# Seven plain chunks instead of six ahead of the halved products, with the making of the activation halves spread anew

## The chip, the core and the metric

The kernel runs on one core of one Trainium2 chip. The metric is the device time of one execution in microseconds (us). A core has a matrix engine (TensorE, "PE" in a profile; its weight loads are "PEld"), a vector engine (VectorE, "DVE"), a scalar engine (ScalarE, "ACT"), GpSimd ("POOL") and a queue engine (SyncE, "SP") from which this kernel issues its transfers. Each engine works through its own list of instructions in order; between engines the program waits on semaphores.

## The reference, cut to what matters

One layer with 512 tokens and a model width of 1024. Four mixers write into a merged activation, and then the part that the change touches follows, a gated feed-forward network with 2816 hidden columns:

```python
x = x + merged @ w_out[l]
hn = rmsnorm(x, ffn_norm_g[l])
gu = hn @ w_up[l]                                   # 1024 -> 2 * 2816
h = jax.nn.silu(gu[..., :FFN_HIDDEN]) * gu[..., FFN_HIDDEN:]
x = x + h @ w_down[l]
return rmsnorm(x, final_norm_g)
```

## The kernel before

Activations lie with their features on the 128 partitions and the 512 tokens along the free axis. To keep single precision at the matmul's faster rate, every operand is split into a high part (a rounding copy on ScalarE, `A.copy`) and a low part (the difference, a subtraction on VectorE), and each product is three matmuls: high times high, high times low, low times high. Weights arrive in chunks of up to 128 x 2048 floats through two buffers named `raw`; while TensorE works on one chunk, ScalarE and VectorE split the next (`hi` and `lo`, or `ahi` and `alo`).

The up projection takes 22 chunks, one for each block of 128 hidden columns, in two parts of eleven (`for part in range(2)`); after each part the matching rows of `w_down` are multiplied in.

The first `N_PLAIN` chunks, six of them, are plain: `mm3` makes the gate product `psg` (tile `m_fg`) and then the up product `psu` (`m_fu`), each with 24 matmuls of 128x512. `glu_up` then scales both (`tg`, `tu`), takes the silu of `tg` on ScalarE, multiplies, and splits the result into `hh` (ScalarE) and `hl` (VectorE), which only the `w_down` products read.

All later chunks are halved: `up_halved` makes the same two products with a Strassen-like scheme from seven products of half the size, each with 12 matmuls of 128x256 (`prod`, names B11, B21, T2, T1, T3, B22 and T4, in this order). They read sums and differences of weight quarters, made by the step `sum` and its fellows in `split_steps`, and sums and differences of activation halves. B11, T2, T3 and T4 all add up in one half `ac` of a PSUM bank (tile `s_fa`); between them ScalarE copies the running sum out (`A.copy(mu[:, h0], ac)` after B11, and again after T2), so T2 may not write before the first copy is done. That copy stands on ScalarE behind the first high part of the next chunk (`emit(st, "ha")`).

The activation halves are made once, by `halves_gen`, during the plain chunks. It has twelve steps, three for each of four values of k. Step A scales two blocks of x2 (`xsa`, `xsb`; VectorE) and copies (`xsp`) and rounds (`xsh`) on ScalarE. Step B makes the differences (two `xst`, two `xsu`) and one low part (`xsl`) on VectorE, and rounds two tiles on ScalarE. Step C makes the other low parts, two for even k and three for odd k. Where the steps stand is set by hand: each plain chunk from the third on takes one (`next(prep)`) between its two products, and then `PREP[j]` more behind its `glu_up`. B11, the first half-size product, reads the last low part of the last step C.

There is no scheduler: the engines' order is the order of the Python code (`tc.manual_schedule()`), and helper calls all carry line 81, so the rows below are told apart by their tiles. The prediction names chunks by j, from 0: the last plain chunk is 5 before.

Of the kernel before, what the change touches and what calls it, by code (L numbers as in the profile page):

```python
# [14 lines left out]
ALU = mybir.AluOpType  # L15
# [41 lines left out]
N_WARM = 8  # L57
N_HALVED = 2
BC_AT = 7
PREP = (0, 1, 2, 1, 2, 2)  # L60
N_PLAIN = 6
W0_PIECES = {0: 1, 1: 3, 4: 2, 6: 2}
S5_PAR = 48
S5_W = S5_PAR + 4 * 256
# [21 lines left out]
def _advance(clock, key, cost):  # L86
    clock[key] = cost + (clock[key] if key == "pe" else max(clock[key], clock["pe"]))
# [3 lines left out]
def hybrid_trunk(ctx: ExitStack, tc: tile.TileContext, a: dict, out: bass.AP):  # L91
# [3 lines left out]
    V = _Paced(nc.vector, lambda n: _advance(clock, "v", 0.09 + 1.04e-3 * n))  # L95
    A = _Paced(nc.scalar, lambda n: _advance(clock, "a", 0.20 + 0.83e-3 * n))
# [16 lines left out]
    def nm_(nm):  # L113
        uid[0] += 1
        return f"{nm}_{uid[0]}"

    def slot(nm):
        return sp.tile([P, T], F32, tag="s", name=nm_(nm))
# [5 lines left out]
    def main_ps(nm):  # L124
        return pm.tile([P, T], F32, tag="mm", name=nm_("m_" + nm))

    def side_ps(nm):
        return pa.tile([P, T], F32, tag="at", name=nm_("s_" + nm))

    def r_(t):  # L130
        return t.bitcast(F32R)

    def split(src, nm, mk=None):
        mk = mk or slot
        hi = mk(nm + "h")
        lo = mk(nm + "l")
        A.copy(r_(hi), src)
        V.tensor_tensor(r_(lo), src, hi, ALU.subtract)
        return r_(hi), r_(lo)
# [13 lines left out]
    for part in range(2):  # L153
        specs += [
            ("w_up", j, 2048) if j < N_PLAIN else ("w_ups", j - N_PLAIN, 2048)
            for j in range(NH // 2 * part, NH // 2 * (part + 1))
# [77 lines left out]
    def emit(steps, *names):  # L234
        for n in names:
            for f in steps.pop(n, ()):
                f()

    def flush(steps):
        for n in ("ha", "la", "sum", "ha2", "la2", "sum4", "hb", "lb", "hc", "lc", "ld"):  # L240
            emit(steps, n)

    def open_chunk():
        c = used[0]
        used[0] += 1
        while len(loaded) < min(len(ready) + N_RAW, len(specs)):
            load_next()
        steps = {}
        if len(ready) < min(c + 2, len(specs)):
            steps = split_steps()  # L250
        return ready[c], steps
# [24 lines left out]
    def mm3(ps, ch, c, nw, acts, k0=0):  # L276
        n = len(acts)
        for k, (ah, al) in enumerate(acts):
            wh, wl = ch.h(k0 + k, c, P, nw), ch.l(k0 + k, c, P, nw)
            PE.matmul(ps, wh, ah, start=k == 0, stop=False)  # L280
            PE.matmul(ps, wh, al, start=False, stop=False)
            PE.matmul(ps, wl, ah, start=False, stop=k == n - 1)
# [90 lines left out]
    def inv_rms(ps, n):  # L373
        def s_(nm):
            return gp.tile([P, n], F32, name=nm_(nm))

        ms = s_("ms")
        V.tensor_scalar(ms, ps, 1.0 / D, EPS, ALU.mult, ALU.add)
        rt = s_("rt")
        A.activation(rt, ps, AF.Sqrt, scale=1.0 / D, bias=epsc)  # L380
        r0 = s_("r0")
        V.reciprocal(r0, rt)
        t = s_("nt")
        V.tensor_tensor(t, r0, r0, ALU.mult)
        V.scalar_tensor_tensor(t, t, -0.5, ms, ALU.mult, ALU.mult)
        r = s_("rr")
        V.scalar_tensor_tensor(r, t, 1.5, r0, ALU.add, ALU.mult)
        return r

    def diags(r, nm):  # L390
        o = []
        for b in range(4):
            dg = sm.tile([P, P], F32, tag="dg", name=nm_("dg"), bufs=4)
            V.tensor_scalar(dg, ident, r[:, b : b + 1], None, ALU.mult)
            o.append(dg)
        return o

    def bcast_rows(dgs, rb):
        ps = side_ps("bc")
        for b in range(4):  # L400
            PE.matmul(ps[:, b * P : (b + 1) * P], ones, dgs[b], start=True, stop=True)
        A.copy(rb, ps)

    def ssq_mm(acc):
        ps = side_ps("ssq")
        for b in range(4):
            PE.matmul(ps[:, b : b + 1], acc[:, b * P : (b + 1) * P], ones[:, 0:1], start=True, stop=True)
        return ps
# [7 lines left out]
    for kt in range(KT):  # L416
        hi, lo = slot("xh"), slot("xl")
# [796 lines left out]
    for c in range(4):  # L1214
        ch = next_chunk()
        for n in range(2):
# [6 lines left out]
            hi, lo = slot("x2h"), slot("x2l")  # L1223
# [7 lines left out]
    def glu_up(psg, psu):  # L1231
        tg, tu = slot("tg"), slot("tu")
        V.tensor_tensor(tg, psg, rb2, ALU.mult)
        A.activation(tg, tg, AF.Silu)
        V.tensor_tensor(tu, psu, rb2, ALU.mult)
        V.tensor_tensor(tu, tu, tg, ALU.mult)
        return split(tu, "h")

# [57 lines left out]
    def up_halved(late):  # L1298
        ch, st = open_chunk()
        pa_, pb_ = side_ps("fa"), main_ps("fb")  # L1300
        ac, b1, b2 = pa_[:, h0], pb_[:, h0], pb_[:, h1]
        mu, cn = slot("mu"), slot("cn")
        prod(ac, ch.ahi, ch.alo, 0, "B11", first=True)
        emit(st, "ha")
        late[0]()
        emit(st, "la")
        A.copy(mu[:, h0], ac)
        prod(b1, ch.ahi, ch.alo, 2, "B21", first=True)
        emit(st, "sum")
        late[1]()  # L1310
        emit(st, "ha2", "la2", "sum4")
        prod(ac, ch.hi, ch.lo, 0, "T2")
        A.copy(mu[:, h1], ac)
        prod(b2, ch.hi, ch.lo, 1, "T1", first=True)
        emit(st, "hb")
        A.copy(cn[:, h0], b2)
        emit(st, "lb")
        prod(ac, ch.hi, ch.lo, 3, "T3")
        V.tensor_tensor(cn[:, h1], ac, cn[:, h0], ALU.add)
        emit(st, "hc", "lc")  # L1320
        prod(b2, ch.hi, ch.lo, 2, "B22")
        V.tensor_tensor(mu, mu, pb_, ALU.add)
        A.activation(mu, mu, AF.Silu)
        flush(st)
        prod(ac, ch.ahi, ch.alo, 1, "T4")
        tu, hi, lo = slot("tu"), slot("hh"), slot("hl")
        hid.append((r_(hi), r_(lo)))

        def high():
            V.scalar_tensor_tensor(tu[:, h0], ac, -1.0, mu[:, h0], ALU.mult, ALU.mult)  # L1330
            V.scalar_tensor_tensor(tu[:, h1], cn[:, h1], -1.0, mu[:, h1], ALU.mult, ALU.mult)
            A.copy(r_(hi), tu)

        def low():
            V.tensor_tensor(r_(lo), tu, hi, ALU.subtract)

        return high, low

    hk = NH // 2
    for part in range(2):  # L1340
        hid = []
        late = (lambda: None,) * 2
        for j in range(hk * part, hk * (part + 1)):
            if j >= N_PLAIN:
                late = up_halved(late)
                continue
            ch, st = open_chunk()
            emit(st, "ha", "la")
            if "sum" not in st:
                flush(st)  # L1350
            psg = main_ps("fg")
            mm3(psg, ch, 0, 256, x2g)
            if j == 1:
                bcast_rows(dgs, rb2)
                hid.append(glu_up(*first))
                prep = halves_gen()
            if j > 1:
                next(prep)
            emit(st, "sum", "ha2", "la2", "sum4", "hb", "lb")
            psu = side_ps("fu") if j < 2 else main_ps("fu")  # L1360
            mm3(psu, ch, P, 256, x2g)
            if j == 0:
                dgs = diags(inv_rms(ssq_mm(acc)[:, 0:4], 4), "r2")
                acc = None
                first = psg, psu
                continue
            hid.append(glu_up(psg, psu))
            for _ in range(PREP[j]):
                next(prep)
            flush(st)  # L1370
        for nt in range(8 - N_HALVED * part):
            if nt == 0:
                ch, st = open_chunk()
                emit(st, "ha")
                late[0]()
                late[1]()
                flush(st)
            else:
                ch = next_chunk()
            ps = main_ps("d")  # L1380
            mm3(ps, ch, 0, P, hid)
            V.tensor_tensor(x2[nt], ps, x2[nt], ALU.add)
            if part:
                acc = sumsq_add(acc, x2[nt])
# [125 lines left out]
def _layout(inp):  # L1510
# [47 lines left out]
    for b, kts in enumerate((4, 2, 4, 4)):  # L1558
# [8 lines left out]
    up = _chunks(wu, 256)  # L1567
    o["w_up"] = up[:N_PLAIN]
    hv = up[N_PLAIN:].reshape(NH - N_PLAIN, P, 2, 4, 2, P).transpose(0, 1, 4, 2, 3, 5)
    o["w_ups"] = np.ascontiguousarray(  # L1570
        np.stack([hv[:, :, 0, 0], hv[:, :, 1, 1], hv[:, :, 0, 1], hv[:, :, 1, 0]], axis=2)
    ).reshape(NH - N_PLAIN, P, 2048)
    wd = f["w_down"][0]
# [21 lines left out]
```

## Time and profile before

| what | value |
|---|---|
| median of three runs | 986.85 us (986.72 to 987.58) |
| the profiled execution, whole | 987.47 us |
| its span, first to last instruction | 985.4 us |
| TensorE busy | 965.4 us, 98% of the span |
| VectorE busy | 661.7 us, 67% |
| ScalarE busy | 411.9 us, 42% |
| mean granted TensorE clock | 0.992 of full |

Busy shares are means over stages that differ. The time at the end is set where the engine that is nearly always busy stands still, so the list of what TensorE waited for is read first, and then the lists of instructions in order of time around that wait. In such a list each row has the start, the duration, the engine, the operation and its tiles as out<-in; what stands in brackets is idle time of that engine just ahead of the row, with the instruction that ended it. Instructions of one engine overlap a little, so that the step from one start to the next is somewhat shorter than a duration.

### The profile page before, as it was taken

The page shows a single profiled execution, that of the slowest core. Times are in us where ns is not written, and L with a number is a line of the kernel's source. Part 1 is how long each engine was busy: PE and PEld are TensorE (multiplying, and loading weights), DVE is VectorE, ACT ScalarE, POOL GpSimd, SP SyncE. Part 2 cuts the span into 40 slices and gives each one's busy share as a digit, 9 for nine tenths or more (in the row PEclk, how much of TensorE's full clock was granted, in tenths as well). Part 3 has the DMA queues.
Part 4 walks back from the last instruction along what each step waited for, and adds up shares of the span by engine and source line. Part 5 has one row for each costly group of instructions (what it writes and reads, how often), then busy time and mean ns, then how long its engine had stood idle before and what let it go on. Part 6 is the DMA issues. An engine that isn't in the chain of part 4 may idle for free.

```text
span 985.4 us, 13841 instructions
## 1 busy us (share of the span) xinstructions
PE 965.4 (98%) x5462; PEld 834.9 (85%) x5462; DVE 661.7 (67%) x1260; ACT 411.9 (42%) x718; POOL 4.3 (0%) x20
## 2 busy tenths in 40 slices
PE   8999999999999999999999999996999999999996
PEld 7887888888888888887888888885998899999886
DVE  6676676688777877945545555579883379997344
ACT  7443533343545344227333334354552235554231
POOL 1000000000000000000000000000000000000000
PEclk9999999999999999999999999999899999999998
DMA  8532222231222213251532332221223223232312
GB/s 274 182 111 97 88 89 88 68 121 37 68 77 72 69 58 111 100 192 65 182 117 96 118 128 85 86 86 44 94 94 118 102 86 129 86 123 74 110 59 86
DMA packets 38696, 100.26 MB, mean 102 GB/s; under 512 B 14222, under 2 KB 22075, under 8 KB 32872
## 3 DMA queue, kind: packets, MB, share of 16 engines
q1 hardware_dynamic: 38632, 99.38, 29.9%
q8 instruction: 43, 0.70, 0.3%
q14 instruction: 21, 0.17, 0.1%
HBM read 94.94 MB, written 4.42 MB: 101 GB/s over the span
## 4 chain that ended last, share of the span: by engine, by line
PE 94%; DVE 3%; ACT 1%; DMA 0%; issue 0%; SPq 0%; DVEq 0%
PE m_g L81 17%; PE m_d L81 12%; PE s_fa L81 9%; PE m_b L81 7%; PE m_fb L81 7%; PE m_qk L81 7%; PE m_sqk L81 4%; PE m_o L81 4%; PE m_v L81 3%; PE m_u L81 3%; PE m_fg L81 3%; PE m_sv L81 2%; PE m_fu L81 2%; PE s_u L81 1%; PE s_fu L81 1%; PE m_gb L81 1%
## 5 line engine op out<-in xcount | busy, mean ns | idle before, releaser
L81 DVE TENSOR_TENSOR lo<-raw,hi 128x1024 fp32r<-128x1024 f32 (+5 forms) x208 | 198.1, 984 | 54.8 <-ACT hi L81 53.9
L81 ACT CAST hi<-raw 128x1024 fp32r<-128x1024 f32 (+5 forms) x208 | 169.4, 858 | 64.3 <-PE m_d L81 30.0
L81 PE MATMUL m_g<-xh,hi 128*128 128x512 f32 x256 | 102.6, 401 | 0.0
L81 PE MATMUL m_g<-xh,lo 128*128 128x512 f32 x256 | 100.0, 391 | 0.3 <-DVE lo L81 0.3
L81 PE MATMUL m_g<-xl,hi 128*128 128x512 f32 x256 | 99.6, 389 | 0.0
L81 PE MATMUL m_d<-hh,hi 128*128 128x512 f32 (+1 forms) x198 | 72.5, 366 | 0.0
L81 PE MATMUL m_d<-hl,hi 128*128 128x512 f32 (+1 forms) x198 | 72.4, 366 | 0.0
L81 PE MATMUL m_d<-hh,lo 128*128 128x512 f32 (+1 forms) x198 | 72.3, 365 | 0.0
L81 ACT ACTIVATE gt<-gt 128x512 f32<-128x512 f32 x32 | 20.2, 631 | 109.7 <-DVE gt L81 109.7
L81 PEld LDWEIGHTS m_g<-xh,lo 128*128 128x128 f32 x256 | 48.0, 188 | 11.3 <-DVE lo L81 1.0
L81 PEld LDWEIGHTS m_g<-xh,hi 128*128 128x128 f32 x256 | 48.1, 188 | 10.9 <-issue 1.0
L81 PEld LDWEIGHTS m_g<-xl,hi 128*128 128x128 f32 x256 | 48.1, 188 | 10.7 <-issue 1.0
L81 DVE TENSOR_TENSOR x<-m_d,x 128x512 f32<-128x512 f32 (+1 forms) x18 | 11.4, 633 | 62.5 <-PE m_d L81 62.5
L81 PE MATMUL s_fa<-xsl,ahi 128*128 128x256 f32 x128 | 36.7, 286 | 8.6 <-DVE xsl L81 8.6
L81 DVE TENSOR_TENSOR raw<-raw 128x512 f32<-128x512 f32 (+1 forms) x48 | 41.8, 870 | 1.6
L81 PEld LDWEIGHTS m_d<-hh,lo 128*128 128x128 f32 x198 | 37.3, 189 | 6.1
L81 PEld LDWEIGHTS m_d<-hh,hi 128*128 128x128 f32 x198 | 37.3, 189 | 6.0
L81 PEld LDWEIGHTS m_d<-hl,hi 128*128 128x128 f32 x198 | 37.4, 189 | 5.9
L81 DVE TENSOR_TENSOR gt<-m_b,gt 128x512 f32<-128x512 f32 x24 | 16.5, 689 | 37.9 <-PE m_b L81 32.8
L81 ACT ACTIVATE prob<-prob,nmx 128x128 f32<-128x128 f32 (+1 forms) x48 | 20.1, 419 | 49.3 <-DVE nmx L81 49.2
L81 PE MATMUL m_qk<-xh,hi 128*128 128x512 f32 x96 | 38.2, 397 | 0.0
L81 PE MATMUL m_qk<-xl,hi 128*128 128x512 f32 x96 | 37.4, 390 | 0.0
(400 smaller groups left out, 2523.7 us busy)
## 6 DMA issues: line engine op xcount, KB each, us to landing
raw<-in_w_g SPq DMA_DIRECT2D x24, 768.0 KB, 4.3
raw<-in_w_in SPq DMA_DIRECT2D x17, 1024.0 KB, 6.8
raw<-in_w_ups SPq DMA_DIRECT2D x16, 1024.0 KB, 4.8
raw<-in_w_down SPq DMA_DIRECT2D x16, 704.0 KB, 4.0
raw<-in_w_up SPq DMA_DIRECT2D x6, 1024.0 KB, 4.8
raw<-in_w_g SPq DMA_DIRECT2D x8, 640.0 KB, 3.9
raw<-in_w_out SPq DMA_DIRECT2D x4, 1024.0 KB, 4.8
x<-in_x SPq DMA_DIRECT2D x8, 256.0 KB, 5.5
```

The costliest lines, as they stand in the source:

```text
L81: return f(out, *args, **kw)
```

## The change

Seven plain chunks stand ahead of the halved ones in place of six, so there are fifteen halved chunks, not sixteen. `PREP` is another table, the steps of `halves_gen` begin in chunk 1 and end in chunk 5, and the low part of h (`hl`) is no longer issued by `glu_up` itself: `glu_up` returns it, and it is issued behind the steps that follow.

```diff
-PREP = (0, 1, 2, 1, 2, 2)
-N_PLAIN = 6
+PREP = (0, 1, 2, 2, 1, 1)
+N_PLAIN = 7
...
         V.tensor_tensor(tu, tu, tg, ALU.mult)
-        return split(tu, "h")
+        hi, lo = slot("hh"), slot("hl")
+        A.copy(r_(hi), tu)
+        hid.append((r_(hi), r_(lo)))
+        return lambda: V.tensor_tensor(r_(lo), tu, hi, ALU.subtract)
...
             if j == 1:
                 bcast_rows(dgs, rb2)
-                hid.append(glu_up(*first))
+                low = glu_up(*first)
                 prep = halves_gen()
-            if j > 1:
+                next(prep)
+                low()
+            elif 1 < j < 6:
                 next(prep)
...
-            hid.append(glu_up(psg, psu))
-            for _ in range(PREP[j]):
+            low = glu_up(psg, psu)
+            for _ in range(PREP[j] if j < 6 else 0):
                 next(prep)
+            low()
             flush(st)
```

So the steps stand as follows (Ak, Bk, Ck for each k; what is in brackets stands between the two products of a chunk, the rest behind its `glu_up`):

| chunk j | before | after |
|---|---|---|
| 1 | A0 | A0 (ahead of the `hl` of chunk 0), B0 |
| 2 | (B0) C0 A1 | (C0) A1 B1 |
| 3 | (B1) C1 | (C1) A2 B2 |
| 4 | (A2) B2 C2 | (C2) A3 |
| 5 | (A3) B3 C3, then the first halved chunk | (B3) C3 |
| 6 | | no step, then the first halved chunk |

VectorE at the last steps, before. It begins with the product of the last plain chunk (5): `tu` and `hl` belong to `glu_up`, the nine rows from `xst` to `xsl` are B3 and C3 less their parts on ScalarE, and `lo_5891` finishes the weights of the first halved chunk:

```order
L81 TENSOR_TENSOR tu_5963<-m_fu_5937,rb_879_5442 128x512
L81 TENSOR_TENSOR tu_5963<-tu_5963,tg_5962 128x512
L81 TENSOR_TENSOR hl_5969<-tu_5963,hh_5968 128x512
L81 TENSOR_TENSOR xst_5972<-xsa_5921 128x256
L81 TENSOR_TENSOR xst_5972<-xsb_5922,xsa_5921 128x256
L81 SCALAR_TENSOR_TENSOR xsu_5973<-xst_5972,xsb_5922 128x256
L81 SCALAR_TENSOR_TENSOR xsu_5973<-xsu_5973,xsb_5922 128x256
L81 TENSOR_TENSOR xsl_5978<-xsb_5922,xsh_5926 128x512
L81 TENSOR_TENSOR xsl_5984<-xst_5972,xsh_5980 128x512
L81 TENSOR_TENSOR xsl_5986<-xsu_5973,xsh_5982 128x512
L81 TENSOR_TENSOR xsl_5988<-xsp_5833,xsh_5928 128x512
L81 TENSOR_TENSOR lo_5891<-raw_5796,hi_5890 128x512 x2
```

The same engine after, from the product of chunk 5, which is no longer the last plain one:

```order
L81 TENSOR_TENSOR tu_5968<-m_fu_5942,rb_879_5442 128x512
L81 TENSOR_TENSOR tu_5968<-tu_5968,tg_5967 128x512
L81 TENSOR_TENSOR xsl_5976<-xst_5930,xsh_5938 128x512
L81 TENSOR_TENSOR xsl_5978<-xsu_5931,xsh_5940 128x512
L81 TENSOR_TENSOR xsl_5980<-xsp_5799,xsh_5894 128x512
L81 TENSOR_TENSOR hl_5974<-tu_5968,hh_5973 128x512
L81 TENSOR_TENSOR alo_5988<-raw_5897,ahi_5987 128x1024
L81 TENSOR_TENSOR raw_5897<-raw_5897 128x2x512
L81 TENSOR_TENSOR raw_5897<-raw_5897 128x512
L81 TENSOR_TENSOR alo_5988<-raw_5897,ahi_5987 128x512
L81 TENSOR_TENSOR raw_5897<-raw_5897 128x512
L81 TENSOR_TENSOR lo_5986<-raw_5897,hi_5985 128x1024
```

The last `xsl` of C3 stands behind the product of chunk 5 in both, but chunk 5 was followed by the first halved chunk and is now followed by chunk 6; the weights of the first halved chunk (`alo`, `raw`, `lo`) now come behind all steps, and `hl` behind the low parts.

ScalarE around the end of the last plain chunk, before (`tg` is its silu, `hh` the high part of its h, `hi_5890` the last weights of the first halved chunk, `ahi_5998` the first of the second, and `mu` the copy that T2 waits for):

```order
L81 ACTIVATE tg_5962<-tg_5962 128x512
L81 CAST hh_5968<-tu_5963 128x512
L81 CAST xsh_5980<-xst_5972 128x512
L81 CAST xsh_5982<-xsu_5973 128x512
L81 CAST hi_5890<-raw_5796 128x512 x2
L81 CAST ahi_5998<-raw_5888 128x1024
L81 COPY mu_6002<-s_fa_6000 128x256
```

And after:

```order
L81 ACTIVATE tg_6048<-tg_6048 128x512
L81 CAST hh_6054<-tu_6049 128x512
L81 CAST hi_5985<-raw_5897 128x512 x2
L81 CAST ahi_6066<-raw_5983 128x1024
L81 COPY mu_6070<-s_fa_6068 128x256
```

The two roundings of step B are gone from this place; the rest stands as it stood, with `mu` behind `hh`, `hi` and `ahi`.

## Rows read from the trace of the kernel before

**Rows 1.** From the page: the span, and its instructions.
```profile
span 985.4 us, 13841 instructions
```
**Rows 2.** What TensorE waited for, whole run: us in total, times, longest us.
```profile
PE s_fa L81 <- DVE xsl L81: 8.6, 1, 8.6
```
**Rows 3.** TensorE in order of time: chunk starts, the gap, a chunk's last matmul.
```profile
669.63 0.39 PE L81 MATMUL m_fu<-x2h,lo 128*128 128x512 f32 x1
669.85 0.39 PE L81 MATMUL m_fg<-x2h,hi 128*128 128x512 f32 x1
...
680.73 0.28 PE L81 MATMUL s_fa<-xsh,ahi 128*128 128x256 f32 x1
...
681.45 0.28 PE L81 MATMUL s_fa<-xsh,ahi 128*128 128x256 f32 x1
690.30 0.58 PE L81 MATMUL s_fa<-xsl,ahi 128*128 128x256 f32 x1 [8.57 <-DVE xsl L81]
...
702.17 0.28 PE L81 MATMUL s_fa<-xsh,ahi 128*128 128x256 f32 x1
...
712.25 0.28 PE L81 MATMUL s_fa<-xsh,ahi 128*128 128x256 f32 x1
```
**Rows 4.** Stretches: length, busy us (count) of PE, PEld, DVE, ACT, POOL; PEclk, DMA, GB/s.
```profile
669.85:680.73 10.88, 10.88 (x49) 9.01 (x48) 9.81 (x16) 5.49 (x10) 0.00 (x0) 1.00 0.18 77
685.00:687.00 2.00, 0.00 (x0) 0.00 (x0) 1.33 (x4) 0.62 (x1) 0.00 (x0) 0.72 0.00 0
693.00:695.00 2.00, 2.00 (x12) 2.00 (x11) 1.97 (x3) 0.00 (x0) 0.00 (x0) 0.50 0.89 360
702.17:712.25 10.08, 10.08 (x86) 10.08 (x85) 9.24 (x14) 5.72 (x11) 0.00 (x0) 1.00 0.28 106
```
**Rows 5.** VectorE in order of time, from chunk 5 to the last step.
```profile
665.38 2.35 DVE L81 TENSOR_TENSOR lo<-raw,hi 128x1024 fp32r<-128x1024 f32 x2
...
670.05 0.69 DVE L81 TENSOR_TENSOR tu<-m_fu,rb 128x512 f32<-128x512 f32 x1 [0.39 <-PE m_fu L81]
670.85 0.69 DVE L81 TENSOR_TENSOR tu<-tu,tg 128x512 f32<-128x512 f32 x1
...
672.84 0.42 DVE L81 TENSOR_TENSOR xst<-xsa 128x256 f32<-128x256 f32 x1
...
675.51 0.68 DVE L81 TENSOR_TENSOR xsl<-xsu,xsh 128x512 fp32r<-128x512 f32 x1
676.12 1.22 DVE L81 TENSOR_TENSOR alo<-raw,ahi 128x1024 fp32r<-128x1024 f32 x1
677.25 0.74 DVE L81 SCALAR_TENSOR_TENSOR xsa<-x,cols,rb 128x512 f32<-128x512 f32 x1
...
678.57 1.95 DVE L81 TENSOR_TENSOR raw<-raw 128x1024 f32<-128x1024 f32 x2
680.44 0.69 DVE L81 TENSOR_TENSOR alo<-raw,ahi 128x512 fp32r<-128x512 f32 x1
...
682.91 0.68 DVE L81 TENSOR_TENSOR tg<-m_fg,rb 128x512 f32<-128x512 f32 x1
...
689.55 0.69 DVE L81 TENSOR_TENSOR xsl<-xsp,xsh 128x512 fp32r<-128x512 f32 x1
```
**Rows 6.** What VectorE waited for from 630 to 702 us: total, times, longest us.
```profile
DVE lo L81 <- ACT hi L81: 5.9, 3, 2.2
DVE hl L81 <- ACT hh L81: 4.1, 6, 0.7
```
**Rows 7.** ScalarE in order of time: the instructions that stand ahead of `mu`.
```profile
671.58 0.62 ACT L81 CAST hh<-tu 128x512 fp32r<-128x512 f32 x1 [1.25 <-DVE tu L81]
...
688.39 1.13 ACT L81 CAST hi<-raw 128x512 fp32r<-128x512 f32 x2
689.43 1.04 ACT L81 CAST ahi<-raw 128x1024 fp32r<-128x1024 f32 x1
691.77 0.37 ACT L81 COPY mu<-s_fa 128x256 f32<-128x256 f32 x1 [1.30 <-PE s_fa L81]
```

## The prediction

> **What bounds the kernel now.** The list of TensorE's waits comes first: the engine is busy nearly all the time, and its one long wait, 8.6 us, is that of `s_fa`, the first halved product, for a low activation half, `xsl` [rows 2]. The list of TensorE in order of time gives the place. Chunk 5 starts at 669.85 and the first halved chunk at 680.73, so a plain chunk takes 10.88 us. Seven matmuls later, at 681.45, TensorE stands still until 690.30; the next two halved chunks start at 702.17 and 712.25 [rows 3]. An undisturbed halved chunk thus takes 10.08 us and the first took 21.44: an excess of **11.36 us**. Of it 690.30 - 681.45 - 0.12 = 8.73 is the gap (0.12 is the step of these matmuls: 10.08 / 84). The other 2.63 comes after the gap: the granted clock was 1.00 in chunk 5, fell during the gap (0.72 in the mean of 685 to 687), was 0.50 at 693 to 695 while TensorE worked without a pause, and 1.00 again from 702.17 on [rows 4]. Half speed is 1.2 of 2.4 GHz.
>
> The Trainium skill, "TensorE: Matmul & The Clock Gate", section "Part 1: The HAM clock gate", says that idleness throttles TensorE to half and that activity releases it; these rows agree.
>
> The list of VectorE tells why the half is late. At 689.55 it does the last `xsl` of C3, and the matmul starts 0.06 us after that ends [rows 5]. VectorE had simply not got through its list: it was busy 9.81 of 10.88 us in chunk 5 [rows 4], and it stood idle for 4.1 us in six waits for `hh` just ahead of `hl` [rows 6].
>
> **The change, part by part.** Times are counted on the trace of before, whose order is the same up to the product of chunk 0.
>
> *The gap and its clock go, if the halves are ready.* Chunk 6 is now plain and runs from 680.73 to 691.61. The product of chunk 5 can start when its last matmul is done. In chunk 4 `tu` started 0.42 us after the last `m_fu` started (669.63 to 670.05), and the second `tu` 0.80 later [rows 3, 5]. So for chunk 5: last matmul 680.51, `tu` 680.93, second `tu` 681.73, then the three `xsl` of C3 at 0.61 each (675.51 to 676.12): done by 684.2, where the first halved product now wants them at 691.6. That is 7.4 us to spare where 8.7 were missing. Is VectorE on time at 680.93? From the `tu` of chunk 4 at 670.05: 0.80, then 0.60, then A3 at 1.32 (677.25 to 678.57) [rows 5], `hl` 0.61, and then it needs ScalarE's `hi`, which stands behind `hh` (671.58 [rows 7]) and three small copies, so that it can begin the two `lo` near 675.0; 2.35 for these, 2.07 for B3 (672.84 to 676.12 is 3.28 for B and two `xsl`, less 1.21), 0.60 for `tg`: 680.0. About 0.9 us to spare, so yes. Both halves of the excess go: **-11.36**.
>
> *A halved chunk becomes a plain one*: 10.88 - 10.08 = **+0.80**. The bytes loaded are the same; VectorE and ScalarE have less to do for it.
>
> The Trainium skill, "Perfetto Trace Analysis", section "Matmuls", holds that larger matmuls are more efficient than smaller ones. Taken alone, that would price this swap at nothing or a gain, and the sum would be 0.80 lower. The rows agree per column (48 x 512 in 10.88 us against 84 x 256 in 10.08) but the halved chunk has an eighth fewer columns, and so the measured 0.80 decides.
>
> *A new wait.* T2 may not write before `mu` has been copied, and on ScalarE `mu` stands behind `hh` of the last plain chunk, two `hi` and one `ahi`. Before, that chain was through long before TensorE woke: `mu` itself waited 1.30 us for TensorE [rows 7]. Now it starts from the end of chunk 6: last `m_fu` at 691.39, `tu` at 691.81, `hh` 1.53 us after that (670.05 to 671.58 [rows 5, 7]) at 693.34; then `hh` 0.62, two `hi` 1.04 (688.39 to 689.43), `ahi` 1.04 and `mu` 0.37 [rows 7]: `mu` is done at 696.4. TensorE has only B11 and B21 to do meanwhile, 24 matmuls at 0.12: T2 could begin at 691.61 + 2.88 = 694.5. So it waits **+1.9**. VectorE must not be late for this `tu`: after C3 (684.2) it has `hl` 0.61, `alo` 1.13 (676.12 to 677.25), the sums 1.87 (678.57 to 680.44), three more rows 2.47 (680.44 to 682.91) and `tg` 0.60 [rows 5]: 690.9, some 0.9 us early. The bounds of this wait: 1.5, if each of the four copies overlaps the next by 0.1, as the two `hi` do with `ahi` (1.13 long, 1.04 apart); 2.8, if VectorE is 0.9 late after all, its reserve lost twice over.
>
> *Behind it* VectorE begins the next `alo` at about 696.0, and T4 waits for its `cn`. An undisturbed halved chunk holds 9.24 us of VectorE work in 10.08 [rows 4]; of the 0.84 to spare a lag of this size uses up nearly all. I take **+0.1**, bounds 0 and 0.8.
>
> *Edits at nothing.* `hl` behind the steps: its readers are the `w_down` products, four halved chunks later, and steps now fill most of the 4.1 us of waiting [rows 6]; without that cover nothing changes for TensorE, which does not read it. A0 in chunk 1: VectorE has slack there. The transfers: the program issues the same loads in the same order, each when the low parts of its buffer's last chunk are done, and TensorE waits for none of them before [rows 2]; the load of the third halved chunk starts when the last `lo` of the first one is done, about when `mu` is (696), and is wanted near 704.
>
> **Sum**: -11.36 + 0.80 + 1.9 + 0.1 = -8.56. The profiled execution took 987.47 us, 2.07 more than its span [rows 1], and 0.62 more than the median of 986.85; the saving lies inside the span, so it is taken off the median: 986.85 - 8.56 = **978.3 us**. With the bounds of the two waits (1.5 + 0 to 2.8 + 0.8) the forecast's own range is 977.8 to 979.9.
>
> **The rivals.**
>
> *No new wait.* If T2 did not have to wait, because `mu` gets through earlier than this chain has it, TensorE would run on: 986.85 - 10.56 = 976.3. For it: before, nothing of the kind is among TensorE's waits [rows 2]. Against it: before, the gap hid this chain, and every row of it has a duration.
>
> *The clock falls again.* The new wait of 1.9 us could do what that of 8.73 did. Its price would be up to the 2.63 paid before: 978.3 + 2.6 = 980.9. Against it: in the one long gap the clock was still high for 4.3 us (a mean of 0.72 between 1.00 and 0.50 puts the fall near 685.9, the last matmul near 681.6) [rows 3, 4], more than twice the new wait.
>
> The page named above would make a gap that is long enough throttle the engine; whether this one is, no row here shows.
>
> *VectorE late at every plain chunk: slower than before.* The steps stand closer now. The fullest list is that from the `tu` of chunk 2 to that of chunk 3: 0.80 + 0.60, A1 1.32, B1 2.07, `hl` 0.61, `lo` 2.35, C1 1.83, `tg` 0.60 [rows 5], together 10.18, and some 0.5 of waiting for `hi`: 10.7 of the 10.88 that TensorE takes. If that waiting were the 2.2 us that it was at its longest before [rows 6], and the list 0.6 longer than its rows, VectorE would fall 2.1 us behind at each of the five boundaries from chunk 2 to 7, and the matmuls that read `lo` would wait there: 978.3 + 5 x 2.1 = 988.8. It decides from 1.7 us at each boundary (8.56 / 5), a list of 12.6 us. Against it: all of these rows have been seen at their lengths, chunks 4 and 5 have shorter lists and give back what chunk 3 loses, and the first 2 us are forgiven: `lo` was done at 667.7 for a chunk that began at 669.85 [rows 3, 5].
>
> *The change doesn't cure the wait* (the first halved chunk waits for something else that I overlook, such as its weights, for as long as before): about 986 to 987.6, no change.
>
> **How the numbers follow.** Forecast 0.77; no new wait 0.07; the clock 0.10; VectorE late 0.03; not cured 0.03. A difference of 0.2% (2.0 us) is about what a measurement of this kernel can tell from none. The first three cases, 0.94, are faster by more than that; the fourth is slower. Of the last, 0.02 falls within 0.2% and 0.01 on a small gain: faster 0.95, same 0.02, slower 0.03. The range takes in the forecast's bounds, the case without a wait and that of the clock: 976.1 to 981.0. Outside lie the last two cases, 0.06, and some tails.
>
> **What would show it.** In the profile after, `s_fa <- xsl` is gone from TensorE's waits; in its place stands one wait of about 1.9 us of `s_fa` for ScalarE's `mu`, near 694.5, and perhaps one below 0.5 us for `cn`. The seventh plain chunk runs from about 680.7 to 691.6, the granted clock stays at 1.00 through both, the second halved chunk starts near 703.6 and the third 10.08 later. A TensorE wait for `lo` or `tu` at the start of chunks 3 to 6 would show the slower rival, a clock of 0.50 behind the new wait the second, and no TensorE wait at all the first. The prediction is wrong if the first halved chunk still waits longer than 4 us for anything.

## The result, and the profile after

The kernel after took **979.50 us** in the median of four runs (978.61 to 980.17), the kernel before 986.99 us in the median of four on the same chip. The ratio is 0.9921, with a 95% interval of 0.9908 to 0.9933: 7.5 us faster by the medians, where 8.56 were forecast, and the whole interval lies below 1. The profiled execution took 980.17 us with a span of 978.4 us.

The first view is the list of what TensorE waited for in the kernel after (total us, times, longest us):

```profile
PE s_u L81 <- ACT hi L81: 2.9, 2, 1.5
PE s_fa L81 <- ACT mu L81: 1.6, 1, 1.6
```

The wait of 8.6 us for `xsl` [rows 2] is gone. In its place stands one of 1.6 us for `mu`. The other row, two waits of `s_u` (the first product of the kernel), lies in the first ten microseconds and comes up again below.

TensorE of the kernel after in order of time (start, duration, operation, idle time ahead of it and what ended that). The rows answer to [rows 3]: start of chunk 6, start of the first halved chunk, last matmul of B21, first of T2, last matmul ahead of T4, T4, and the second halved chunk.

```profile
682.34 0.39 PE L81 MATMUL m_fg<-x2h,hi 128*128 128x512 f32 x1
...
693.22 0.28 PE L81 MATMUL s_fa<-xsh,ahi 128*128 128x256 f32 x1
...
695.97 0.28 PE L81 MATMUL m_fb<-xsh,alo 128*128 128x256 f32 x1
697.87 0.39 PE L81 MATMUL s_fa<-xsh,hi 128*128 128x256 f32 x1 [1.62 <-ACT mu L81]
...
703.61 0.28 PE L81 MATMUL m_fb<-xsh,lo 128*128 128x256 f32 x1
703.74 0.29 PE L81 MATMUL s_fa<-xsh,ahi 128*128 128x256 f32 x1
...
705.17 0.28 PE L81 MATMUL s_fa<-xsh,ahi 128*128 128x256 f32 x1
```

Chunk 6 takes 693.22 - 682.34 = 10.88 us as a plain chunk. The first halved chunk runs through to B21 without a pause, then stands still ahead of T2. Chunks 6 and 7 together took 712.25 - 680.73 = 31.52 us before, both halved [rows 3]; after, one plain and one halved, they take 705.17 - 682.34 = 22.83. That is 8.69 us less.

The stretches of the kernel after (length; busy us and count of PE, PEld, DVE, ACT, POOL; granted clock; share and GB/s of the transfers), as in [rows 4]: chunk 6, the wait, the time behind it, and the second halved chunk.

```profile
682.34:693.22 10.88, 10.88 (x49) 9.01 (x48) 9.88 (x13) 4.04 (x6) 0.00 (x0) 1.00 0.12 47
...
696.00:698.00 2.00, 0.38 (x4) 0.18 (x3) 1.91 (x4) 2.00 (x5) 0.00 (x0) 1.00 0.00 0
698.00:700.00 2.00, 2.00 (x17) 2.00 (x18) 1.97 (x2) 0.71 (x2) 0.00 (x0) 1.00 0.71 213
705.17:715.25 10.08, 10.08 (x86) 10.08 (x85) 9.31 (x14) 5.77 (x11) 0.00 (x0) 1.00 0.30 104
```

The granted clock stays at 1.00, that is 2.4 GHz, through the wait and behind it. Before, it fell to 0.50 [rows 4].

VectorE of the kernel after, at the products of chunk 5 and chunk 6, and at the last `xsl` of C3:

```profile
682.54 0.69 DVE L81 TENSOR_TENSOR tu<-m_fu,rb 128x512 f32<-128x512 f32 x1 [0.47 <-PE m_fu L81]
...
685.15 0.69 DVE L81 TENSOR_TENSOR xsl<-xsp,xsh 128x512 fp32r<-128x512 f32 x1
...
693.42 0.69 DVE L81 TENSOR_TENSOR tu<-m_fu,rb 128x512 f32<-128x512 f32 x1 [0.80 <-PE m_fu L81]
```

VectorE now waits for TensorE at both products; it is on time with 0.47 and 0.80 us to spare. The last `xsl` is done at 685.84, 7.4 us ahead of the chunk that wants it.

ScalarE of the kernel after, from the last `hh` of a plain chunk to `mu`, the rows that answer to [rows 7]:

```profile
694.94 0.62 ACT L81 CAST hh<-tu 128x512 fp32r<-128x512 f32 x1 [1.59 <-DVE tu L81]
695.47 1.14 ACT L81 CAST hi<-raw 128x512 fp32r<-128x512 f32 x2
696.51 1.04 ACT L81 CAST ahi<-raw 128x1024 fp32r<-128x1024 f32 x1
697.46 0.36 ACT L81 COPY mu<-s_fa 128x256 f32<-128x256 f32 x1
```

B11 is finished at 694.8, so `mu` could have been copied then. It stands behind `hh`, two `hi` and `ahi`, which have no pause between them, and T2 follows 0.05 us after it ends.

### Where the missing microsecond is

The up projection begins with the first `m_fg`, at 613.58 in the trace of before and 615.18 in that of after. From there to the end of the span it is 371.8 us before and 363.2 after: 8.6 less, the forecast. What the profiled run lost again, 1.6 us, it lost ahead of the up projection, where the change alters nothing. TensorE at the start of the kernel after:

```profile
7.16 0.40 PE L81 MATMUL s_u<-xh,lo 128*128 128x512 f32 x1
8.95 0.50 PE L81 MATMUL s_u<-xh,hi 128*128 128x512 f32 x1 [1.40 <-ACT hi L81]
...
12.00 0.63 PE L81 MATMUL s_u<-xh,lo 128*128 128x512 f32 x1
...
20.75 0.39 PE L81 MATMUL m_u<-xh,hi 128*128 128x512 f32 x1
```

and its stretches there (columns as above):

```profile
10.00:12.00 2.00, 2.00 (x7) 1.58 (x7) 2.00 (x4) 1.94 (x4) 0.00 (x0) 0.69 1.07 411
12.00:14.00 2.00, 2.00 (x6) 1.62 (x5) 2.00 (x4) 1.94 (x4) 0.00 (x0) 0.50 1.02 405
```

TensorE begins at full pace, runs out of weights after six matmuls, stands still for 1.40 us, and soon after that works at half the clock for some 3 us. The pause alone is not what costs the time, as the last section shows. The same place in the trace of before:

```profile
6.35 0.80 PE L81 MATMUL s_u<-xh,hi 128*128 128x512 f32 x1 [1.58 <-ACT hi L81]
...
19.23 0.39 PE L81 MATMUL m_u<-xh,hi 128*128 128x512 f32 x1
```

Here the first matmuls go at half pace (the next starts 0.59 us later, those behind it 0.43 us apart), the weights are there when they are wanted, nothing runs dry, and the second chunk of weights is reached at 19.23, not 20.75.

### The profile page after: what moved, and what is told of

Read it like the earlier page. It is cut to its first block, busy times and chain, and to the rows that moved or that the text cites. A ratio compares the mean times of both kernels' runs of the same rounds, so it can differ in the third digit from the quotient of the medians.

```text
span 978.4 us, 13757 instructions
## 1 busy us (share of the span) xinstructions
PE 963.7 (99%) x5426; PEld 831.3 (85%) x5426; DVE 656.8 (67%) x1253; ACT 409.1 (42%) x712; POOL 4.3 (0%) x20
## 4 chain that ended last, share of the span: by engine, by line
PE 96%; DVE 2%; ACT 1%; DMA 1%; issue 0%; SPq 0%; DVEq 0%
PE m_g L81 17%; PE m_d L81 12%; PE s_fa L81 9%; PE m_b L81 7%; PE m_qk L81 7%; PE m_fb L81 6%; PE m_sqk L81 4%; PE m_o L81 4%; PE m_fg L81 4%; PE m_v L81 3%; PE m_u L81 3%; PE m_fu L81 3%; PE m_sv L81 2%; PE s_u L81 1%; PE s_fu L81 1%; PE m_gb L81 1%
## 5 line engine op out<-in xcount | busy, mean ns | idle before, releaser
L81 DVE TENSOR_TENSOR raw<-raw 128x512 f32<-128x512 f32 (+1 forms) x45 | 39.1, 870 | 1.6
L81 PE MATMUL m_qk<-xh,lo 128*128 128x512 f32 x96 | 37.4, 390 | 0.0
```

What stands on the lines that cost most here:

```text
L81: return f(out, *args, **kw)
```

## The experiments

The second column is the median of each run, and its ratio is to the kernel before timed beside it on the same chip. The runs stood on three chips, on which the kernel before took 987.15, 988.16 and 987.61 us in the median, so that kernels are better compared by their ratios than by their medians. "Stretch" is the time from the first `m_fg` to the end of the span in the profiled run, which leaves the start out. The kernel after in its own trace: wait for `mu` 1.62 us, stretch 363.2 us; the kernel before: 371.8 us.

| run | median us | ratio to before, 95% interval | span us | first m_fg | stretch us |
|---|---|---|---|---|---|
| again | 979.49 | 0.9918 (0.9905 to 0.9932) | 978.4 | 615.21 | 363.2 |
| e1_seven_alone | 982.54 | 0.9947 (0.9934 to 0.9960) | 978.4 | 613.29 | 365.1 |
| e2_spread_alone | 983.69 | 0.9968 (0.9956 to 0.9979) | 981.7 | 613.38 | 368.3 |
| e3_low_in_place | 983.26 | 0.9959 (0.9945 to 0.9974) | 984.1 | 615.34 | 368.8 |
| e4_mu_first | 978.45 | 0.9910 (0.9897 to 0.9924) | 977.7 | 615.26 | 362.4 |
| e5_wait_plus4 | 983.71 | 0.9960 (0.9945 to 0.9975) | 981.5 | 613.27 | 368.2 |
| e6_wait_plus8 | 985.45 | 0.9979 (0.9970 to 0.9988) | 983.0 | 612.90 | 370.1 |
| e7_longer_warm | 977.89 | 0.9901 (0.9888 to 0.9913) | 976.3 | 613.81 | 362.5 |
| e8_low_alone | 982.20 | 0.9942 (0.9926 to 0.9958) | 979.1 | 613.22 | 365.9 |
| e9_after_warm | 979.12 | 0.9910 (0.9894 to 0.9927) | 977.4 | 614.18 | 363.2 |

### The kernel after once more

> The changed kernel as it is, timed once more beside the kernel before. Theory: everything the change does lies between chunk 6 and chunk 8 of the up projection, where the two traces differ by 8.7 us; the further 1.6 us by which the profiled run of after lags lies in its first 20 us, in a part that the change does not touch, and is chance. Then the median is 978 to 979, the saving 8 to 8.8 us, and in this trace the first plain chunk starts earlier than in the first trace of after, or the same late start is seen in a run of before. Rival: the late start belongs to the changed program; then the median is near 980 and this trace again shows about 1.6 us more of TensorE waits in the first 20 us than any trace of before.

Nothing is edited. The time, the wait for `mu` (1.6 us) and the stretch repeat. The median of 979.49 lies above the 978 to 979 of the theory. The late start came again: a pause of 1.37 us at 9.00, a clock of 0.60 from 10 to 12 us, and `m_u` at 20.78. So this run does not exclude the rival that the late start belongs to the changed program. Against it stand other runs below: ahead of the up projection `e1_seven_alone`, `e5_wait_plus4`, `e6_wait_plus8` and `e8_low_alone` have the same instructions as the kernel after, and they reach `m_u` at 18.50 to 18.92.

### Seven plain chunks alone

The kernel before with two numbers and a condition changed; steps and low parts stand as before.

```diff
-PREP = (0, 1, 2, 1, 2, 2)
-N_PLAIN = 6
+PREP = (0, 1, 2, 1, 2, 2, 0)
+N_PLAIN = 7
...
-            if j > 1:
+            if 1 < j < 6:
                 next(prep)
```

> Seven plain chunks alone: the old table of steps (none in chunk 6) and the low part of h at its old place. Theory: the wait for xsl goes, since chunk 6 gives it 10.9 us, but VectorE gets to the product of chunk 6 about 2.0 us late (six waits of 0.69 for hh come back, and the weights of the first halved chunk stand behind B3 and C3), and the copy mu with it: the wait of T2 is 3.9 us instead of 1.6, and the time 2.0 to 2.5 above the changed kernel, about 981, if the clock holds. Rival (the extra chunk is all that counts): within 0.5 us of the changed kernel.

TensorE ahead of T2, in this kernel's trace:

```profile
697.94 0.39 PE L81 MATMUL s_fa<-xsh,hi 128*128 128x256 f32 x1 [3.57 <-ACT mu L81]
```

and the stretches of and behind that wait:

```profile
696.00:698.00 2.00, 0.06 (x1) 0.07 (x1) 1.91 (x4) 2.00 (x5) 0.00 (x0) 1.00 0.00 0
698.00:700.00 2.00, 2.00 (x17) 2.00 (x18) 1.97 (x2) 0.74 (x2) 0.00 (x0) 1.00 0.66 168
```

In this trace the seventh chunk alone brings 6.7 of the 8.6 us (371.8 - 365.1), close to what the theory had; the wait is a little shorter than its 3.9. Without the other edits VectorE was on time for the product of chunk 5 (it waited 0.54 us for TensorE) and did that of chunk 6 at 693.50, 1.97 us later than the kernel after does, counted from the first `m_fg`. All of that lateness goes into the wait for `mu`: 3.57 - 1.62 = 1.95, and 365.1 - 363.2 = 1.9. The clock held at 1.00 through this wait. In the other four runs the time is 1.2 to 3.3 us longer, with a mean clock of 0.994 to 0.996 in place of 0.997; they have no trace, so whether the clock fell behind this wait or in the start isn't shown. The traced run is the fastest of the five: by the medians, beside the same runs of the kernel before, the seventh chunk alone brings 4.6 us (987.15 - 982.54) where the kernel after brings 7.7 (987.15 - 979.49).

### The steps and the low parts alone

The kernel after with six plain chunks.

```diff
-N_PLAIN = 7
+N_PLAIN = 6
```

> The new table and the late low part of h alone, with six plain chunks: steps begin in chunk 1, C3 still stands behind the product of chunk 5, and the first halved chunk follows. Theory: VectorE has the last xsl at 686.3 on the clock of the trace before (tu of chunk 5 at 683.9, three xsl), so the gap at the first halved product is 4.8 us, not 8.7; nothing is paid for a plain chunk; the clock may fall just before the end of the gap. The time is 4 us below before without a fall of the clock missed in full (983), up to 6.6 below (980.3) if the clock holds. Rival (spreading does nothing without the chunk): within 0.5 us of before.

TensorE in the first halved chunk:

```profile
686.72 0.58 PE L81 MATMUL s_fa<-xsl,ahi 128*128 128x256 f32 x1 [5.20 <-DVE xsl L81]
```

and the stretches of this wait and behind it:

```profile
684.00:686.00 2.00, 0.00 (x0) 0.00 (x0) 1.90 (x5) 1.24 (x4) 0.00 (x0) 0.82 0.00 0
...
690.00:692.00 2.00, 2.00 (x11) 2.00 (x10) 1.97 (x3) 0.00 (x0) 0.00 (x0) 0.50 0.84 344
```

The wait shrinks from 8.57 to 5.20 us, 3.37 less, and the stretch by 3.5: the clock falls as before and is paid for in full. With six chunks neither of the two orders tried removes the wait. The two halves add up to 6.7 + 3.5 = 10.2, and together they bring 8.6: with the seventh chunk there is no wait for `xsl` left that the new order could shorten. In the traces it is then worth the 1.9 us of the wait for `mu` alone; by the medians it is 3.1 (7.7 - 4.6).

### The low part of h back in its place

The kernel after; the end of `glu_up` is as it was.

```diff
-        return lambda: V.tensor_tensor(r_(lo), tu, hi, ALU.subtract)
+        V.tensor_tensor(r_(lo), tu, hi, ALU.subtract)
+        return lambda: None
```

> The changed kernel with one part undone: hl stands again right behind hh, so that VectorE waits 0.69 us for it in each chunk; seven plain chunks and the new table stay. The prediction costs this edit at nothing. Theory A (VectorE's slack takes most of it): in the trace of after, VectorE had 0.79, 0.47 and 0.80 us of idle time ahead of the products of chunks 4, 5 and 6 and none ahead of that of chunk 3; 0.69 more in each list leaves it some 0.5 us late at chunk 6, the wait of T2 is 2.1 us, the time 0.5 us above the changed kernel. Rival B (what the prediction says, nothing): wait 1.6, same time. Rival C (it is this edit that keeps VectorE on time): the lateness adds up over five chunks to 2 us or more, the wait of T2 is over 3.5 us, the time 2 us or more above the changed kernel.

What VectorE waited for from 618 to 699 us in this kernel:

```profile
DVE lo L81 <- ACT hi L81: 5.4, 4, 2.2
DVE hl L81 <- ACT hh L81: 4.9, 7, 0.7
```

and in the kernel after, in the same stretch:

```profile
DVE tu L81 <- PE m_fu L81: 4.0, 4, 1.9
DVE lo L81 <- ACT hi L81: 3.0, 4, 1.6
DVE hl L81 <- ACT hh L81: 0.7, 1, 0.7
```

In place, each `hl` stands right behind the `hh` that it subtracts, and VectorE waits 0.69 us for it, seven times. Moved, it waits once. That alone is 4.2 us. Together with longer waits for `hi` (2.4) it is more than the 4.0 us that VectorE had in hand ahead of its products, and VectorE comes to the product of chunk 6 2.5 us late (696.13; the last `m_fu` starts at 693.16). So T2:

```profile
700.68 0.58 PE L81 MATMUL s_fa<-xsh,hi 128*128 128x256 f32 x1 [4.27 <-ACT mu L81]
```

and the clock:

```profile
698.00:700.00 2.00, 0.00 (x0) 0.00 (x0) 1.59 (x3) 2.00 (x4) 0.00 (x0) 0.88 0.00 0
700.00:702.00 2.00, 1.32 (x6) 1.32 (x7) 1.88 (x3) 1.15 (x3) 0.00 (x0) 0.50 0.43 53
```

So `hl` in its old place costs TensorE a good deal, as rival C had it. The stretch is 5.5 us longer than after (984.1 - 615.34 against 978.4 - 615.18): 2.65 of wait, and 2.9 lost by work at half the clock. Three of the six runs were long (984.07 to 986.12, mean clock 0.991 to 0.992), three were shorter (982.15 to 982.45, 0.995 to 0.996): the wait is there each time by its order, the fall of the clock probably not, but only the profiled run has a trace.

### The low part alone, with the old table

The kernel after, with seven plain chunks and the old table of steps.

```diff
-PREP = (0, 1, 2, 2, 1, 1)
+PREP = (0, 1, 2, 1, 2, 2, 0)
...
                 low = glu_up(*first)
                 prep = halves_gen()
-                next(prep)
                 low()
...
-            for _ in range(PREP[j] if j < 6 else 0):
+            for _ in range(PREP[j]):
```

> Seven plain chunks, the old table of steps, but hl behind the steps that follow (so the kernel after without the new table). Theory (both edits are needed): with the old table and hl in place VectorE was on time for the product of chunk 5 (it waited 0.54 us there) and 1.97 us late for that of chunk 6, since chunk 5 alone holds B3 and C3; hl behind them saves only the 0.69 us wait of that chunk, so it is still about 1.3 late, T2 waits 1.62 + 1.3 = 2.9 us for mu, and the stretch from the first row of the up projection to the end is about 363.2 + 1.3 = 364.5 us. Rival (the low part is the whole of it, the table does nothing): T2 waits 1.6 us and the stretch is 363.2. Other rival (the low part does nothing here): 3.6 and 365.1, as with seven chunks alone.

T2 in this kernel, and the stretches from its wait on:

```profile
697.13 0.39 PE L81 MATMUL s_fa<-xsh,hi 128*128 128x256 f32 x1 [2.84 <-ACT mu L81]
```

```profile
696.00:698.00 2.00, 0.87 (x5) 0.87 (x6) 1.91 (x3) 1.60 (x3) 0.00 (x0) 0.89 0.16 25
698.00:700.00 2.00, 2.00 (x12) 2.00 (x11) 1.93 (x4) 0.23 (x1) 0.00 (x0) 0.50 0.87 319
```

The wait is 2.84 us as the theory had it (2.9): VectorE waited 1.33 us for the product of chunk 5, so it had time in hand there, and lost it in chunk 5, which holds B3 and C3 in the old table. The stretch is 2.7 us longer than after, not 1.3: the clock fell here too, and that is the other 1.4. So of the new order neither half does it alone. By the ratios the kernel with neither half is just clear of the kernel after, and that with the new table alone well clear; the interval of this one overlaps with it, so that here only the trace tells them apart. With seven chunks the wait for `mu` is 3.57 us with neither, 4.27 with the new table alone, 2.84 with the moved low part alone, and 1.62 with both. The new table leaves VectorE 4.0 us to spare in all, and waits of 0.69 us in every chunk are more than it can bear; the moved low part takes them away.

### The copy for T2 first

The kernel after; in the first halved chunk `mu` is copied right behind B11. For this, in the last plain chunk the two `hi` go ahead of `glu_up`, and its `hh` and `hl` behind that copy. The core of it, in `up_halved`:

```diff
         prod(ac, ch.ahi, ch.alo, 0, "B11", first=True)
+        if first:
+            A.copy(mu[:, h0], ac)
         emit(st, "ha")
...
-        A.copy(mu[:, h0], ac)
+        if not first:
+            A.copy(mu[:, h0], ac)
```

> The changed kernel with the new wait taken away: at the first halved chunk alone ScalarE copies mu right behind B11, ahead of ahi and of hh of chunk 6, and the last two hi of the first halved chunk stand ahead of the silu of chunk 6; the same work otherwise. Theory: mu is what T2 waits for, so the wait of 1.6 us at T2 is gone; VectorE, whose list is nearly as long as a halved chunk, may give back up to 0.8 of it at T4 or at the product before. The time is 0.8 to 1.6 us below the changed kernel, near 977.5. Rival (T2 waits for something else that ends at the same time, a transfer or VectorE): the same time as the changed kernel, within 0.4.

TensorE in the first halved chunk waits twice more, where it did not in the kernel after:

```profile
700.90 0.38 PE L81 MATMUL m_fb<-xsh,hi 128*128 128x256 f32 x1 [0.25 <-ACT cn L81]
...
702.95 0.38 PE L81 MATMUL s_fa<-xsh,ahi 128*128 128x256 f32 x1 [0.36 <-DVE cn L81]
```

The wait for `mu` is gone, so its cause was the order on ScalarE. Some of it comes back, 0.61 us in two waits for `cn`: VectorE has the same list to get through, and TensorE now comes to its results sooner. Ahead of the first `cn` ScalarE stood idle for 1.34 us until VectorE had made a sum of weights; ahead of the second stands the `hl` that was put off. 0.8 us of 1.62 remain in the stretch, 1.0 in the median; the intervals of the two ratios overlap.

### The wait made longer

The kernel after; in the first halved chunk alone ScalarE makes copies that nobody reads ahead of `mu`, four in the first run, eight in the second.

```diff
+        for _ in range(4 if first else 0):
+            A.copy(cn, x2[0])
         A.copy(mu[:, h0], ac)
```

> The changed kernel with four copies of 128x512 that nobody reads put ahead of mu on ScalarE, at the first halved chunk alone: the wait of T2 is 2.1 us longer, some 3.7 us, and the result unchanged. Theory: the clock holds, as it did over the wait of 3.57 us with seven chunks alone; the stretch from the first chunk of the up projection to the end is 2.1 us longer, or up to 2.6 if VectorE gets late by it too. Rival (the clock falls again with a gap well under that of before): 2.1 + up to 2.6 longer, and a granted clock of 0.50 behind the wait.

ScalarE ahead of `mu` in this kernel, T2, and the stretches of its wait:

```profile
695.54 2.56 ACT L81 COPY cn<-x 128x512 f32<-128x512 f32 x4
```

```profile
698.43 0.58 PE L81 MATMUL s_fa<-xsh,hi 128*128 128x256 f32 x1 [4.09 <-ACT mu L81]
```

```profile
696.00:698.00 2.00, 0.00 (x0) 0.00 (x0) 1.97 (x2) 1.90 (x4) 0.00 (x0) 0.59 0.61 160
698.00:700.00 2.00, 1.57 (x7) 1.57 (x8) 1.88 (x4) 0.90 (x3) 0.00 (x0) 0.50 0.87 365
```

The copies made the wait 2.47 us longer, and the stretch 5.0: the clock fell, at a cost of 2.5 us. The theory that it would hold at a wait of this length is wrong, and the rival is right.

> The same with eight such copies: the wait of T2 is 4.2 us longer, some 5.8 us. Theory: the clock falls, as it did in the wait of 5.2 us with the spread alone; the stretch to the end is 4.2 + 2.2 to 2.6 us longer than with the changed kernel. Rival (the clock holds as long as TensorE has just been working without a pause): 4.2 longer and a granted clock of 1.00 throughout.

T2 with eight copies:

```profile
700.66 0.58 PE L81 MATMUL s_fa<-xsh,hi 128*128 128x256 f32 x1 [6.69 <-ACT mu L81]
```

5.07 us more of wait, 6.9 more of stretch: the fall costs 1.8 here. The clock read 1.00 up to 698 us and 0.54 from 698 to 700.

### A longer warm-up at the start

```diff
-N_WARM = 8
+N_WARM = 20
```

In `e7_longer_warm` this is added to the kernel with the copy first, in `e9_after_warm` to the kernel after. The matmuls of the warm-up are done ahead of the first product and nobody reads them.

> The kernel with mu first, and 20 idle matmuls at the start in place of 8. In the traces so far the first chunk took one of two courses: TensorE starts on it at 5.8 to 6.4 us at half clock and reaches the second chunk at 18.9 to 19.2; or it gets an early first piece, runs dry for 1.4 us near 7.6 to 9.0, the granted clock falls to 0.5 near 10.5, and the second chunk starts at 20.8. Theory: the second course comes from running dry; if TensorE is kept at idle matmuls until about 7.6 us, it does not run dry, the clock does not fall, the second chunk starts at 18.8 to 19.6 in every run, and the runs lie within 1 us of each other, near 977.6. Rival (the course is decided elsewhere, by the transfers): the second chunk starts at 20.8 in this trace too, or the runs spread over 1.5 us or more as before.

> The kernel after with N_WARM 20 in place of 8 and nothing else. Theory (the part of the forecast that was missing lies in the start, where TensorE runs dry at the first weights and then at half the clock): the first product starts near 8.4 us at full pace and does not wait, the first m_u row stands near 19.4 us in place of 20.75, the stretch from the up projection to the end stays 363.2, and the median is about 979.5 - 1.0 = 978.5 us, with runs closer together than 1.5 us. Rival (the start is not where it went): the median stays at 979.5, and the first m_fg row at 615.2.

TensorE at the start of `e7_longer_warm`:

```profile
0.99 7.68 PE L319 MATMUL s_warm<-ones 128*128 128x128 f32 x40 [0.99 <-POOL epsc L338]
8.43 0.48 PE L81 MATMUL s_u<-xh,hi 128*128 128x512 f32 x1
```

The first product begins later, at full pace, and does not run dry; the granted clock is 1.00 from 6 to 14 us. In `e9_after_warm` it begins at 7.64 and still waits twice, for 0.28 and 0.26 us, which its theory had not foreseen; the clock is 1.00 there too. `m_u` stands at 19.41 and 19.77 in these two kernels; without the longer warm-up it stands at 20.90 and 20.75. So the profiled runs gain 1.5 and 1.0 us ahead of the up projection; the stretch stays as it was. The medians move by less, 0.56 (978.45 to 977.89) and 0.4 (979.5 to 979.12), but the kernels of each pair were not timed beside each other; by the ratios it is 0.0009 in the one, and 0.0008 to 0.0011 in the other, that is 0.8 to 1.1 us. The intervals of the ratios overlap. The runs of `e7_longer_warm` lie within 1.4 us, a little more than expected, those of `e9_after_warm` within 0.6, those of the kernel after, eight in two sets, within 2.4. This fits a longer warm-up that cuts the late starts off, and the early ones too, since it holds back a first product that can do better without it (`m_u` at 18.50 in `e6_wait_plus8`); two traces do not show it for every run. That the start varies and that its late course costs 1.5 to 2.4 us against the other traces with the short warm-up is shown; that it is all of what the median lacks is not, since most runs have no trace. `e7_longer_warm` is the fastest kernel of this study, with a ratio of 0.9901 where the kernel after has 0.9921 and 0.9918.

## Why the prediction was right, and where not

**The gap and the clock, -11.36**: right. Both are gone; the last low half is there 7.4 us early, the figure that the prediction had.

**The plain chunk, +0.80**: right, 10.88 us in place of 10.08.

**The wait for `mu`, +1.9**: right in place, cause and size. T2 starts 697.87 - 695.97 - 0.12 = 1.78 us late, and `mu` comes 4.46 us after the last `m_fu` starts (697.46 to 693.00), where the chain had some 4.6. The run with `mu` first shows that this order is the cause.

**Behind it, +0.1**: not seen where it was expected. T4 follows the matmul ahead of it by 0.13 us. The first halved chunk takes 705.17 - 693.22 = 11.95 us, which is 1.87 more than an undisturbed one; the 0.09 that go beyond T2's 1.78 lie in the first step behind the wait, 0.22 us in place of 0.12.

**The sum, -8.56**: 8.69 between the two chunk starts, 8.6 from the up projection to the end.

**Taken off the median**: here lies the error of 1.2 us in the forecast of 978.3. This step took for granted that all the rest would repeat. In the two profiled runs of the kernel after the first 20 us did not: `m_u` came 1.5 us later than in the run of before, and behind the pause stood a stretch at half the clock. Since the kernel's own runs differ by up to 2.4 us, a saving that is known to 0.1 us gives a median that is known to about 1. That 979.5 still lies in the forecast's own range of 977.8 to 979.9 is luck: its upper end was meant for longer waits in the halved chunk, and those did not come.

**Edits at nothing, the moved `hl`**: wrong. The step was right that its readers come much later, and that TensorE does not read it. It knew the 4.1 us that VectorE waits ahead of `hl` [rows 6], and held that they make no difference to TensorE. It asked who waits for the moved instruction, and did not follow what a late VectorE holds up: the product, then `hh`, then `mu`, then T2. In its old place `hl` holds VectorE for 0.69 us in each plain chunk; back there, it makes VectorE 2.5 us late, and the stretch 5.5 us longer. The sum did not suffer, because it priced VectorE with the order after, in which these waits are gone, and found 0.9 us to spare where 0.47 and 0.80 were measured.

**The clock rival**: it did not happen, in any of the three traces with a wait of 1.62 us (`e9_after_warm` is the third), but the reason against it was weak. The prediction said that the clock had held for 4.3 us in the gap before, more than twice the new wait. In the run with four copies it fell 2.0 us after the last matmul: the mean of 0.59 from 696 to 698, between 1.00 and 0.50, puts the fall near 696.4, and the wait began at 694.34. A wait of 2.84 us, the length that the prediction had as the upper bound of this wait, brought a fall too. So its price there was not 0.9 us more but some 2.3, and the upper end of 979.9 for the forecast's own range was too low by the clock that goes with such a wait.

**VectorE late**: no wait of TensorE for `lo` or `tu` appeared. The run with `hl` in place shows how far this rival was: VectorE 2.5 us late, felt by TensorE at one place alone, T2, and the kernel still faster than before, at a ratio of 0.9959.

## What to carry to other kernels

Before an edit in an in-order queue is priced at nothing, ask both who waits for the instruction and what it waits for; here a subtraction right behind the other engine's rounding held up its whole queue for 0.69 us each time, and a few places later it did so once in seven. When a long wait is removed, follow the next engine's order from the work that now ends last: the copy that frees an accumulator stood behind three unrelated ones, and this was the one new wait. A saving that is read from one stage should be tested from the start of that stage, since other parts of the kernel can vary, as the start did here, by as much as a term of the sum.

## What the runs showed of the hardware

How long TensorE may stand still before the clock falls is not one number here. The rows are one trace each, but for the first, which repeats in three; the times of the falls are estimates from the means of the stretches.

| gap us | run | granted clock | fall, us after TensorE had stopped |
|---|---|---|---|
| 1.62 | kernel after | 1.00 throughout | |
| 2.84 | e8_low_alone | fell to 0.50 | 3.3, that is 0.4 after it had begun to work again |
| 3.57 | e1_seven_alone | 1.00 throughout | |
| 4.09 | e5_wait_plus4 | fell to 0.50 | 2.0 |
| 4.27 | e3_low_in_place | fell to 0.50 | 3.1 |
| 5.20 | e2_spread_alone | fell to 0.50 | 3.8 |
| 6.69 | e6_wait_plus8 | fell to 0.50 | 4.2 |
| 8.57 | kernel before | fell to 0.50 | 4.2 |

The price of a fall, apart from the wait itself, was between 1.4 and 2.9 us. The Trainium skill, "TensorE: Matmul & The Clock Gate", section "Part 1: The HAM clock gate", says that the monitor which sets the clock runs freely and does not start with the kernel, so that the point of a change differs from run to run. The rows are in keeping with it, since the length of the gap does not tell by itself when or whether the clock falls; what sets it in each run they do not show.

At the start the same instructions take one of three courses. In `before`, `e1_seven_alone` and `e2_spread_alone` the first matmuls are slow and never short of weights, and `m_u` stands at 18.92 to 19.23. In seven other traces with the short warm-up TensorE runs dry for 1.07 to 1.90 us near 7 to 9 us. In four of these (`after`, `again`, `e3_low_in_place`, `e4_mu_first`) the clock then falls to 0.50, and `m_u` stands at 20.75 to 20.91. In the other three (`e5_wait_plus4`, `e6_wait_plus8`, `e8_low_alone`) it stays at 1.00, and `m_u` stands at 18.50 to 18.89, the earliest of all. So the dry pause does not bring the fall by itself, and without the fall it costs nothing that can be seen. From `e8_low_alone`, whose pause of 1.89 us is longer than that of the kernel after:

```profile
8.68 0.51 PE L81 MATMUL s_u<-xh,hi 128*128 128x512 f32 x1 [1.89 <-ACT hi L81]
...
18.89 0.39 PE L81 MATMUL m_u<-xh,hi 128*128 128x512 f32 x1
```

Here it is 10.21 us from the end of the pause to `m_u`, and 11.80 in the kernel after (8.95 to 20.75): the stretch at half the clock costs the 1.6 us. Why the clock fell in four of these traces and not in three stays open.

In the trace of before, the matmuls of the first 3 us start 0.43 us apart, half the full pace, while the row of the stretch from 6 to 8 us gives a granted clock of 1.00. The trace's first record of the clock begins at 10.04 us, just where the step falls from 0.43 to 0.23; ahead of it there is no record, and the column shows 1.00 all the same. So at the very start of a span the pace of the matmuls tells more than that column.
